# A third seven-product pair in each SwiGLU unit, eight in each half of the last product, and gate biases by DMA

## The chip, the cores and the metric

The kernel runs on one core of a Trainium2 chip. The metric is the device time of one execution in microseconds; of several runs the median is given.

## The reference

One decoder block on `x` of 256 rows (tokens) and 2048 columns in fp32. Its first part, a token mixer, isn't touched by the change except for one gate row. The second part is a SwiGLU feed-forward layer, with `D_FF` = 5632:

```
mod = silu(c) @ w_ada + b_ada
shift1, scale1, gate1, shift2, scale2, gate2 = split(mod, 6)
h = rms_norm(x, norm1_gain) * (1 + scale1) + shift1
x = x + gate1 * mixing_sublayer(h, ...)
h = rms_norm(x, norm2_gain) * (1 + scale2) + shift2
gate, up = split(h @ w_ffn_in, 2)
x = x + gate2 * ((silu(gate) * up) @ w_ffn_out)
```

`w_ffn_in` is 2048 x 11264, `w_ffn_out` 5632 x 2048, `w_ada` 2048 x 12288.

## The kernel before, in words

**Products in three matmuls.** Each fp32 operand is split into a high part (a cast) and a low part (what the cast left over). A product of a 128 x 128 block of activations with a 128 x 512 block of weights is three matmuls into one PSUM bank (`mm3`, L164 to L166): high by high, high by low, low by high. Weights stream from HBM by SP's DMA queue into `raw` (four buffers); ACT casts `whi`, DVE subtracts for `wlo` (four buffers each; L158 and L159 in `load_weights`, L1276 and L1277 in `load_pair`). A buffer of `whi` is free when PE's last matmul on it is done.

**SwiGLU units.** The columns of `w_ffn_in` are done in 11 units of 512 gate and 512 up columns each. The inner dimension has 16 blocks, or eight *pairs*; there are two token tiles. An ordinary pair is (2 blocks) x (gate, up) x (2 tiles) = 8 block products, 24 matmuls. Units 1 to 7 (`FAST`) go through `fast_products`, in the order of `PAIRS`, where a 1 marks a pair that is done with seven block products in the manner of Strassen and Winograd, 21 matmuls. Such a *fast* pair needs sums of weights (four subtractions on DVE, L1280, and split as well) and sums of activations (made once, by `sums_of_h2`). Four of its seven products go to shared banks `p1`, `p5`, `p7`, `p6`, which all fast pairs of a unit add into; behind the last fast pair `u`, `first` and `third` are formed from them (one copy on ACT, four operations on DVE), and `merge` adds them to the unit's four banks with four additions on DVE (L1311). `merge(0)` comes two pairs behind the last fast one and `merge(1)` three pairs behind; where no such pair is left, both come at the end. A unit has four banks of its own and four of the other kind; units alternate between `acc` and `misc`.

**Behind a unit** come its sigmoids on ACT (L1387), the gate products on DVE (L1388) and the products with the up half (L1399). The result is transposed on PE in the next unit behind its pair 0 (`turn`, L1115) and split (L191, L192 and their neighbours), so that it is a left operand of the last product.

**The last product** takes the 44 blocks of the result by `w_ffn_out`. Columns 0 to 1023 go by `OUT_A`, 22 pairs of which six are fast; columns 1024 to 2047 by `OUT_B`, 14 pairs of which six are fast, and then ordinary `block` calls for the rest. The left sums of the fast pairs come from three units (`OUT_UNITS`), by `sums_of_unit` (L1429 to L1439) at `hooks`, positions in `OUT_A`. `LOOK` is how many pairs ahead weights are loaded in `OUT_A`.

**Background work.** The gate rows `gate1` and `gate2` are made beside the products: `ada_segment_steps` loads pieces of `w_ada`, `mac` multiplies and adds them on DVE (L286 for the first, L288 for the others), and `rows_of` adds the bias, loaded by a DMA into a scratch row (L970), with four additions on DVE (L971), splits, sums over partitions by matmuls with ones (L985, L986) and copies. How many steps are taken for each pair or block is set by `RATE_MID` (gate1), `RATE_FFN` and, in the last product, `RATE_OUT` (gate2). `flush` takes all that is left.

**Order.** A scheduler sets the order on each engine from the program's order and priorities; `prio()` moves work ahead. Each engine then takes its instructions in that order.

Of the kernel before, what the change touches and what calls it, by code (L numbers as in the profile page):

```python
# [10 lines left out]
F32 = mybir.dt.float32  # L11
# [20 lines left out]
SEG_SHIFT1, SEG_SCALE1, SEG_GATE1, SEG_SHIFT2, SEG_SCALE2, SEG_GATE2 = range(6)  # L32
RATE_IN, RATE_MID, RATE_FFN = 0.8, 0.6, 0.65
RATE_OUT = 2.5
LOOK = 3
DEFER = 4
# [8 lines left out]
FAST = range(1, 8)  # L45
OUT_UNITS = (4, 5, 6)
OUT_A = tuple((p, 0) for p in range(7)) + tuple(x for i in range(6) for x in ((8 + i, 1), ((7, 14, 15, 16, 17, 18)[i], 0))) + (
    (19, 0), (20, 0), (21, 0))
OUT_B = ((0, 0), (1, 0)) + tuple(x for i in range(6) for x in ((8 + i, 1), (2 + i, 0)))
PAIRS = ((0, 0), (1, 0), (6, 1), (2, 0), (7, 1), (3, 0), (4, 0), (5, 0))  # L50
RANK = 16
# [25 lines left out]
def trunk(ctx: ExitStack, tc: tile.TileContext, I, out):  # L77
# [204 lines left out]

    def ada_mac(acc, raw, k):
        c = csil[:, k : k + 1]
        if k == 0:
            nc.vector.tensor_scalar(acc, raw, c, None, op0=ALU.mult)  # L286
        else:
            nc.vector.scalar_tensor_tensor(acc, raw, c, acc, op0=ALU.mult, op1=ALU.add)  # L288
# [69 lines left out]
    def mac():  # L358
        acc, j, k, raw, done = macs.pop(0)
        with tc.issue_after(state["split"].ins):  # L360
            ada_mac(acc[j], raw, k)
        if done is not None:
            after.append(done)

    def ada_segment_steps(acc, seg, done):


        for k in range(KC):
            for j in range(2):
                while len(macs) >= len(ring["tags"]):  # L370
                    mac()
                raw = araw([P, 2 * NB])
                c0 = seg * D + j * 2 * NB
                with prio():
                    nc.sync.dma_start(raw, w_ada[k * P : (k + 1) * P, c0 : c0 + 2 * NB])
                macs.append((acc, j, k, raw, done if (k, j) == (KC - 1, 1) else None))
                yield
# [587 lines left out]
    def rows_of(name, seg, acc):  # L965

        quarters = [a[:, c : c + NB] for a in acc for c in (0, NB)]
        for j, q in enumerate(quarters):
            br = scr([1, NB])
            nc.sync.dma_start(br, I["b_ada"][:, seg * D + j * NB : seg * D + (j + 1) * NB])  # L970
            nc.vector.tensor_add(q[0:1, :], q[0:1, :], br)  # L971
            yield
        for _ in range(4):
# [211 lines left out]
    def norm2_turn(t, xs):  # L1185
# [8 lines left out]
        for j, ps in enumerate(banks):  # L1194
            hf = S(f"T6", [P, 4, P]) if (j, t) == (3, 0) else scr([P, 4, P])
            h2_raw[j, t] = hf
# [171 lines left out]
    for i in range(NFF):  # L1368
# [54 lines left out]
    KF = 4 * NFF  # L1423
    CUT = KF - 14
    w_fo = I["w_ffn_out"]
    out_sums = {}

    def sums_of_unit(n):
# [5 lines left out]
        sums_of(sf, [full[:, :, t * P : (t + 1) * P] for t in range(NT)], slice(0, 4, 2), slice(1, 4, 2))  # L1434
        hi, lo = (S(f"H{2 + 2 * n + i}", [P, 4, 2, P], F32R) for i in range(2))
        nc.scalar.copy(hi, sf)
        nc.vector.tensor_tensor(lo, sf, hi.bitcast(F32), op=ALU.subtract)
        for m in range(2):
            out_sums[2 * e + m] = [(hi[:, j, m, :], lo[:, j, m, :]) for j in range(4)]  # L1439
# [62 lines left out]
```

## Time and profile before

| | |
|---|---|
| median of 3 runs | 1597.8 us (1597.12 to 1598.16) |
| profiled execution | 1597.22 us, of which the span is 1595.4 us |
| TensorE (PE) busy | 1582.0 us, 99% of the span |
| VectorE (DVE) busy | 1275.5 us, 80% |
| ScalarE (ACT) busy | 837.6 us, 53% |
| DMA | 395.97 MB, 248 GB/s in the mean |
| unit 1 begins, last product begins (from the trace) | at some 918 us and 1353 us of the span |

PE is TensorE's matmuls, PEld its weight loads; DVE is VectorE, ACT ScalarE, POOL GpSimd, SP SyncE, which issues the DMAs. L12 is line 12 of the kernel before. A row of a group reads: line, engine, operation, output and inputs with shape, count, busy time and mean ns of one, idle time ahead of it and who ended that. A row of a timeline gives start and duration in us. A row of stretches gives the busy time of each engine.

### The profile page before, as it was taken

What the parts mean: (1) busy time and instruction counts of PE and PEld (TensorE: products, weight loads), DVE (VectorE), ACT (ScalarE), POOL (GpSimd) and SP (SyncE); (2) the same over time, 40 slices, a digit from 0 to 9 for tenths busy, and PEclk for the clock granted to TensorE, in tenths of its full rate; (3) what the DMA queues carried; (4) which work ended last, traced back from release to release, by engine and by line L of the source; (5) the groups of instructions that cost most, each with busy time, mean ns of one, the idle gap of its engine ahead of it and who ended that gap; (6) DMA issues with size and microseconds to landing.
All of it is one profiled execution on the core that took longest, in us unless ns stands there. A gap on an engine that the chain in (4) does not pass through costs nothing.

```text
span 1595.4 us, 20167 instructions
## 1 busy us (share of the span) xinstructions
PE 1582.0 (99%) x7272; PEld 1308.2 (82%) x7272; DVE 1275.5 (80%) x1523; ACT 837.6 (53%) x1184; POOL 5.3 (0%) x14
## 2 busy tenths in 40 slices
PE   8999999999999999999999999999999999999998
PEld 7878888888888888888887888888888888778887
DVE  6889995888878787878756688888887677988884
ACT  5654449775754434444446655555454443554552
POOL 1000000000000000000000000000000000000000
PEclk9999999999999999999999999999999999999999
DMA  9999997667778889989766466556657889667664
GB/s 339 365 326 320 332 302 245 214 189 257 247 258 280 297 301 314 311 289 310 228 192 210 149 196 195 192 184 193 205 183 226 281 302 314 203 196 225 212 204 140
DMA packets 194596, 395.97 MB, mean 248 GB/s; under 512 B 12914, under 2 KB 27928, under 8 KB 194496
## 3 DMA queue, kind: packets, MB, share of 16 engines
q1 hardware_dynamic: 194096, 394.60, 75.0%
q8 instruction: 57, 0.93, 0.2%
q14 instruction: 43, 0.35, 0.1%
q10 hardware_dynamic: 176, 0.07, 0.0%
q0 software_dynamic: 224, 0.01, 0.0%
HBM read 392.53 MB, written 2.10 MB: 247 GB/s over the span
## 4 chain that ended last, share of the span: by engine, by line
PE 85%; DMA 5%; DVE 5%; ACT 3%; issue 2%; SPq 0%; ACTq 0%; DVEq 0%
PE acc L166 21%; PE acc L165 21%; PE acc L164 20%; PE misc L164 6%; PE misc L166 6%; PE misc L165 6%; DVE wlo L159 1%; ACT whi L158 1%; DMA AR<-w_ada 1%; DVE ada L288 1%; DMA raw<-w_br_gla 1%; DMA raw<-w_ffn_out 1%; PE acc L434 1%; DMA raw<-w_in 1%; PE misc L800 1%
## 5 line engine op out<-in xcount | busy, mean ns | idle before, releaser
L158 ACT CAST whi<-raw 128x1024 fp32r<-128x1024 f32 x362 | 368.6, 1022 | 412.2 <-PE acc L166 264.9
L159 DVE TENSOR_TENSOR wlo<-raw,whi 128x1024 fp32r<-128x1024 f32 x362 | 425.6, 1183 | 186.0 <-ACT whi L158 184.4
L164 PE MATMUL acc<-whi,H 128*128 128x512 f32 x1308 | 511.9, 392 | 1.2 <-ACT H L446 0.8
L165 PE MATMUL acc<-wlo,H 128*128 128x512 f32 x1308 | 510.9, 391 | 0.8 <-DVE wlo L159 0.7
L166 PE MATMUL acc<-whi,H 128*128 128x512 f32 x1308 | 509.8, 390 | 0.4 <-DVE H L453 0.4
L166 PEld LDWEIGHTS acc<-whi,H 128*128 128x128 f32 x1308 | 245.3, 188 | 52.9 <-DVE H L453 1.6
L164 PEld LDWEIGHTS acc<-whi,H 128*128 128x128 f32 x1308 | 245.5, 188 | 52.3 <-ACT H L446 1.3
L165 PEld LDWEIGHTS acc<-wlo,H 128*128 128x128 f32 x1308 | 245.7, 188 | 51.3 <-DVE wlo L159 1.7
L1276 ACT CAST whi<-raw 128x1024 fp32r<-128x1024 f32 (+1 forms) x184 | 179.2, 992 | 134.5 <-PE acc L166 68.0
L1277 DVE TENSOR_TENSOR wlo<-raw,whi 128x1024 fp32r<-128x1024 f32 (+1 forms) x184 | 205.2, 1145 | 19.8 <-ACT whi L1276 18.8
L164 PE MATMUL misc<-whi,H 128*128 128x512 f32 x246 | 96.1, 391 | 0.0
L165 PE MATMUL misc<-wlo,H 128*128 128x512 f32 x246 | 95.8, 389 | 0.0
L166 PE MATMUL misc<-whi,H 128*128 128x512 f32 x246 | 95.8, 389 | 0.0
L164 PE MATMUL acc<-whi,A 128*128 128x512 f32 x222 | 87.1, 394 | 0.5 <-ACT whi L1276 0.4
L165 PE MATMUL acc<-wlo,A 128*128 128x512 f32 x222 | 86.7, 390 | 0.8 <-DVE wlo L159 0.8
L166 PE MATMUL acc<-whi,A 128*128 128x512 f32 x216 | 84.3, 390 | 0.0
L288 DVE SCALAR_TENSOR_TENSOR ada<-AR,csil,ada 128x1024 f32<-128x1024 f32 x59 | 74.8, 1278 | 3.6 <-DMA AR<-w_ada 3.6
L165 PEld LDWEIGHTS misc<-wlo,H 128*128 128x128 f32 x246 | 46.2, 188 | 9.7 <-DVE wlo L1277 0.2
L166 PEld LDWEIGHTS misc<-whi,H 128*128 128x128 f32 x246 | 46.2, 188 | 9.5
L164 PEld LDWEIGHTS misc<-whi,H 128*128 128x128 f32 x246 | 46.2, 188 | 9.5
L164 PEld LDWEIGHTS acc<-whi,A 128*128 128x128 f32 x222 | 41.7, 188 | 9.6 <-ACT whi L1276 1.1
L165 PEld LDWEIGHTS acc<-wlo,A 128*128 128x128 f32 x222 | 41.7, 188 | 9.6 <-DVE wlo L159 1.1
(428 smaller groups left out, 1927.6 us busy)
## 6 DMA issues: line engine op xcount, KB each, us to landing
raw<-w_in SPq DMA_DIRECT2D x205, 512.0 KB, 4.8
raw<-w_ffn_in SPq DMA_DIRECT2D x176, 512.0 KB, 4.2
raw<-w_ffn_out SPq DMA_DIRECT2D x88, 512.0 KB, 4.8
AR<-w_ada SPq DMA_DIRECT2D x79, 512.0 KB, 5.1
raw<-w_out SPq DMA_DIRECT2D x32, 512.0 KB, 4.8
KC<-w_ada SPq DMA_DIRECT2D x30, 512.0 KB, 6.2
OS<-w_ada SPq DMA_DIRECT2D x16, 512.0 KB, 6.9
KD<-w_ada SPq DMA_DIRECT2D x16, 512.0 KB, 5.8
```

Source lines behind the costliest of these rows:

```text
L158: state["cast"] = nc.scalar.copy(hi[:, :n, :], raw[:, :n, :])
L159: state["split"] = nc.vector.tensor_tensor(lo[:, :n, :], raw[:, :n, :], hi[:, :n, :].bitcast(F32), op=ALU.subtract)
L164: nc.tensor.matmul(ps, lh, rh, start=start, stop=False, skip_group_check=seeded)
L165: nc.tensor.matmul(ps, lh, rl, start=False, stop=False, skip_group_check=seeded)
L166: state["mm"] = nc.tensor.matmul(ps, ll, rh, start=False, stop=stop, skip_group_check=seeded)
L288: nc.vector.scalar_tensor_tensor(acc, raw, c, acc, op0=ALU.mult, op1=ALU.add)
L434: state["warm"] = nc.tensor.matmul(ps, ones_r, wide, start=True, stop=True)
L800: nc.tensor.matmul(ps[:n, t * N_GLA + h, :].rearrange("p (s l) -> p s l", l=L), at(f, h, t)[:, :n], odd(at(f, h, t)), start=True, stop=True,)
L1276: nc.scalar.copy(hi[:, :n, :], src)
L1277: state["split"] = nc.vector.tensor_tensor(lo[:, :n, :], src, hi[:, :n, :].bitcast(F32), op=ALU.subtract)
```

## The change

Each fast unit gets a third fast pair (pair 5), and the fast pairs stand at positions 2, 4 and 6 of 0 to 7 instead of 2 and 4. `OUT_UNITS` gets a fourth unit; `OUT_A` and `OUT_B` have eight fast pairs each, `OUT_B` now covers 32 of the 44 blocks, and the rest of the third and fourth column blocks goes by ordinary blocks as before. The left sums are put into other tiles, some of them in pieces, and are made at positions 0, 2, 6 and 9 of `OUT_A` instead of 1, 2 and 4; `flush` moves from position 7 to 4. The sums of h2 get those of pair 5 and stand ahead of unit 0's gate products. For both gates the accumulators are set to zero by GpSimd and their row 0 is filled with the bias by DMA; the first multiply then also adds, and the four bias additions go. `RATE_FFN` goes from 0.65 to 0.75, `LOOK` from 3 to 2. PE's matmuls go from 7106 to 7073, DVE's instructions from 1525 to 1600 in the program.

```diff
-RATE_IN, RATE_MID, RATE_FFN = 0.8, 0.6, 0.65
+RATE_IN, RATE_MID, RATE_FFN = 0.8, 0.6, 0.75
-LOOK = 3
+LOOK = 2
...
-OUT_UNITS = (4, 5, 6)
-OUT_A = tuple((p, 0) for p in range(7)) + tuple(x for i in range(6) for x in ((8 + i, 1), ((7, 14, 15, 16, 17, 18)[i], 0))) + (
-    (19, 0), (20, 0), (21, 0))
-OUT_B = ((0, 0), (1, 0)) + tuple(x for i in range(6) for x in ((8 + i, 1), (2 + i, 0)))
-PAIRS = ((0, 0), (1, 0), (6, 1), (2, 0), (7, 1), (3, 0), (4, 0), (5, 0))
+OUT_UNITS = (3, 4, 5, 6)
+OUT_A = tuple((p, 0) for p in range(5)) + tuple(x for i in range(8) for x in ((6 + i, 1), ((5, *range(14, 21))[i], 0))) + ((21, 0),)
+OUT_B = tuple((p, int(6 <= p < 14)) for p in (0, 1, 6, 2, 7, 8, 3, 9, 4, 10, 11, 5, 12, 14, 13, 15))
+PAIRS = ((0, 0), (1, 0), (5, 1), (2, 0), (6, 1), (3, 0), (7, 1), (4, 0))
...
-    def ada_mac(acc, raw, k):
+    def ada_mac(acc, raw, k, zero=True):
         c = csil[:, k : k + 1]
-        if k == 0:
+        if k == 0 and zero:
...
+    def biased(acc, seg):
+        for j, a in enumerate(acc):
+            nc.gpsimd.memset(a, 0.0)
+            with prio():
+                nc.sync.dma_start(a[0:1, :], I["b_ada"][:, seg * D + j * 2 * NB : seg * D + (j + 1) * 2 * NB])
+        return acc
...
-        for j, q in enumerate(quarters):
-            br = scr([1, NB])
-            nc.sync.dma_start(br, I["b_ada"][:, seg * D + j * NB : seg * D + (j + 1) * NB])
-            nc.vector.tensor_add(q[0:1, :], q[0:1, :], br)
-            yield
...
-                acc = [S(f"T{4 + j}", [P, 2 * NB]) for j in range(2)]
-                yield from ada_segment_steps(acc, seg, rows_of("gate1", seg, acc))
+                acc = biased([S(f"T{4 + j}", [P, 2 * NB]) for j in range(2)], seg)
+                yield from ada_segment_steps(acc, seg, rows_of("gate1", seg, acc), False)
...
-        acc = halves(S("ada", [P, D]))
-        yield from ada_segment_steps(acc, SEG_GATE2, rows_of("gate2", SEG_GATE2, acc))
+        acc = biased(halves(S("ada", [P, D])), SEG_GATE2)
+        yield from ada_segment_steps(acc, SEG_GATE2, rows_of("gate2", SEG_GATE2, acc), False)
...
     def sums_of_h2():
         out = {}
-        sf = S("KC", [P, 4, 2, P])
+        sf = S("AR1", [P, 4, P])
+        sums_of(sf.rearrange("p s (n d) -> p s n d", n=1), [h2_raw[2, t] for t in range(NT)], slice(2, 3), slice(3, 4))
+        hl = S("AR0", [P, 2, 4, P], F32R)
+        nc.scalar.copy(hl[:, 0], sf)
+        nc.vector.tensor_tensor(hl[:, 1], sf, hl[:, 0].bitcast(F32), op=ALU.subtract)
+        out[5] = [(hl[:, 0, j, :], hl[:, 1, j, :]) for j in range(4)]
+        sf = S("AR1", [P, 4, 2, P])
...
+        if i == 0:
+            h2s = sums_of_h2()
         sgs = []
...
-        if i == 0:
-            h2s = sums_of_h2()
...
-    CUT = KF - 14
+    CUT = 2 * len(OUT_B)
...
+    rooms = [S(f"H{2 + j}", [P, 4, 2, P], F32R) for j in range(6)]
...
-        hi, lo = (S(f"H{2 + 2 * n + i}", [P, 4, 2, P], F32R) for i in range(2))
-        nc.scalar.copy(hi, sf)
-        nc.vector.tensor_tensor(lo, sf, hi.bitcast(F32), op=ALU.subtract)
+        homes = []
+        for part in range(2):
+            own = act[e][part][:, 0:4:2, P:T]
+            if n < 3:
+                rest = [(rooms[2 * n + part][:, 0:3], slice(1, 4))]
+            else:
+                rest = [(rooms[2 * j + part][:, 3:4], slice(1 + j, 2 + j)) for j in range(3)]
+            homes.append([(own, 0)] + rest)
+        for part in range(2):
+            for (dst, c), (hi, _) in zip(homes[part], homes[0]):
+                if part == 0:
+                    nc.scalar.copy(dst, sf[:, c])
+                else:
+                    nc.vector.tensor_tensor(dst, sf[:, c], hi.bitcast(F32), op=ALU.subtract)
...
-    hooks = {at: (lambda n=n: sums_of_unit(n)) for n, at in enumerate((1, 2, 4))}
-    hooks[7] = flush
+    hooks = {at: (lambda n=n: sums_of_unit(n)) for n, at in enumerate((0, 2, 6, 9))}
+    hooks[4] = flush
...
-    REST = 2 * len(OUT_B)
-    block(o[0], act_at, w_fo, REST, KF, 2 * NB, go_on=True, seeded=True)
+    block(o[0], act_at, w_fo, CUT, KF, 2 * NB, go_on=True, seeded=True)
...
-    block(pss, act_at, w_fo, REST, CUT, n * NB, go_on=True, more=True, seeded=True)
```

More of the change, by code (lines that the diff above doesn't have):

```diff
@@ L358, in mac, with ada_segment_steps @@
     def mac():
-        acc, j, k, raw, done = macs.pop(0)
+        acc, j, k, raw, done, zero = macs.pop(0)
         with tc.issue_after(state["split"].ins):
-            ada_mac(acc[j], raw, k)
+            ada_mac(acc[j], raw, k, zero)
         if done is not None:
             after.append(done)
-    def ada_segment_steps(acc, seg, done):
+    def biased(acc, seg):
[4 more added lines that the diff above has]
+        return acc
+    def ada_segment_steps(acc, seg, done, zero=True):
         for k in range(KC):
@@ L375, in ada_segment_steps @@
                     nc.sync.dma_start(raw, w_ada[k * P : (k + 1) * P, c0 : c0 + 2 * NB])
-                macs.append((acc, j, k, raw, done if (k, j) == (KC - 1, 1) else None))
+                macs.append((acc, j, k, raw, done if (k, j) == (KC - 1, 1) else None, zero))
                 yield
@@ L1194, in norm2_turn @@
         for j, ps in enumerate(banks):
-            hf = S(f"T6", [P, 4, P]) if (j, t) == (3, 0) else scr([P, 4, P])
+            hf = S(("KC", "T6")[j - 2], [P, 4, P]) if t == 0 and j >= 2 else scr([P, 4, P])
             h2_raw[j, t] = hf
@@ L1434, in sums_of_unit @@
         sums_of(sf, [full[:, :, t * P : (t + 1) * P] for t in range(NT)], slice(0, 4, 2), slice(1, 4, 2))
-        hi, lo = (S(f"H{2 + 2 * n + i}", [P, 4, 2, P], F32R) for i in range(2))
-        nc.scalar.copy(hi, sf)
-        nc.vector.tensor_tensor(lo, sf, hi.bitcast(F32), op=ALU.subtract)
-        for m in range(2):
-            out_sums[2 * e + m] = [(hi[:, j, m, :], lo[:, j, m, :]) for j in range(4)]
+        homes = []
[12 more added lines that the diff above has]
+                    nc.vector.tensor_tensor(dst, sf[:, c], hi.bitcast(F32), op=ALU.subtract)
+        for m in range(2):
+            views = []
+            for part in range(2):
+                v = [homes[part][0][0][:, m, :]]
+                for dst, _ in homes[part][1:]:
+                    v += [dst[:, j, m, :] for j in range(dst.shape[1])]
+                views.append(v)
+            out_sums[2 * e + m] = list(zip(*views))
     state["rate"] = RATE_OUT
-    hooks = {at: (lambda n=n: sums_of_unit(n)) for n, at in enumerate((1, 2, 4))}
-    hooks[7] = flush
+    hooks = {at: (lambda n=n: sums_of_unit(n)) for n, at in enumerate((0, 2, 6, 9))}
+    hooks[4] = flush
     o = fast_products(w_fo, 0, NB, OUT_A, act_at, out_sums, acc_bank, misc_bank, ("AR0", "AR1"), hooks)
```

## The prediction

> **What bounds the kernel now.** I read the page of the profile first, from its head to the chain that ended last.
>
> ```profile
> span 1595.4 us, 20167 instructions
> PE 1582.0 (99%) x7272; PEld 1308.2 (82%) x7272; DVE 1275.5 (80%) x1523; ACT 837.6 (53%) x1184; POOL 5.3 (0%) x14
> PEclk9999999999999999999999999999999999999999
> PE 85%; DMA 5%; DVE 5%; ACT 3%; issue 2%; SPq 0%; ACTq 0%; DVEq 0%
> ```
>
> PE is busy in 99% of the span at an unthrottled clock, and the chain is PE's in 85%. A matmul taken out is therefore worth its full issue time, as long as PE is fed; a stall put in costs its full length. Next I read PE itself: the chain of waits through the SwiGLU units, where each unit transposes its predecessor's result right behind its own pair 0, then PE's timeline at such a place, and PE's waits from 1200 us on.
>
> ```profile
> 1052.95 0.87 PE misc L1115 x8
> 1096.02 0.88 PE acc L1115 x8
> ...
> 1269.65 0.87 PE misc L1115 x8
> 1314.07 0.87 PE misc L1115 x8
> ...
> 1052.79 1.03 PE L1115 MATMUL misc<-ident,scr 128*128 128x128 f32 x8
> ...
> PE misc L985 <- ACT T L980: 0.8, 1, 0.8
> PE acc L164 <- ACT whi L1276: 0.4, 1, 0.4
> ```
>
> A fast unit takes 1096.02 - 1052.95 = 43.07 us and an ordinary one 1314.07 - 1269.65 = 44.42. Fast units have two pairs of 21 matmuls and six of 24, 186 in all; ordinary ones have 192. Less the 0.87 of transposes, that is 42.20/186 = 43.55/192 = 0.227 us a matmul. Two sorts of unit with the same quotient means that neither stalls. The two waits are all that PE shows in the last 395 us, both in the last product.
>
> What the change leans on is DVE, so I asked for the busy time in unit 3 and in two stretches at the start of the last product, and for the groups by form.
>
> ```profile
> 1004.40:1047.45 43.05, 43.05 (x196) 35.73 (x195) 36.16 (x43) 22.36 (x25) 0.00 (x0) 1.00 0.61 197
> 1350.00:1400.00 50.00, 48.92 (x221) 38.95 (x219) 46.12 (x60) 24.42 (x32) 0.00 (x0) 1.00 0.64 208
> 1400.00:1450.00 50.00, 49.45 (x216) 40.29 (x216) 44.40 (x50) 28.89 (x32) 0.00 (x0) 1.00 0.68 212
> ...
> L1277 DVE TENSOR_TENSOR wlo<-raw,whi 128x1024 fp32r<-128x1024 f32 x129 | 153.3, 1220 | 12.0 <-ACT whi L1276 11.1
> L1280 DVE TENSOR_TENSOR AR<-raw,AR 128x512 f32<-128x512 f32 x24 | 16.5, 687 | 0.3
> L971 DVE TENSOR_TENSOR ada<-ada,scr 1x512 f32<-1x512 f32 x4 | 2.6, 673 | 0.0
> L1251 DVE TENSOR_TENSOR AR<-AR,AR 128x256 f32<-128x256 f32 x6 | 2.5, 416 | 0.0
> L1432 DVE TENSOR_TENSOR AR<-T,T 128x1024 f32<-128x1024 f32 x2 | 2.4, 1216 | 0.0
> ```
>
> After the engine sums the columns are PE, PEld, DVE, ACT. DVE is busy 36.2 of 43.05 us in a unit; in the last product 46.1 and 44.4 of 50, and there PE loses 1.1 and 0.55 us.
>
> **Matmuls removed.** Each further fast pair takes three matmuls away. Seven units gain one each: 7 x 3 x 0.227 = -4.8 us. The last product goes from 6 + 6 to 8 + 8: 4 x 3 x 0.227 = -2.7 us. [...]
>
> **DVE inside a unit.** Here are DVE's and ACT's own rows around the end of unit 3.
>
> ```profile
> 1046.18 0.69 DVE L1399 TENSOR_TENSOR scr<-scr,misc 128x512 f32<-128x512 f32 x1
> 1046.79 1.22 DVE L1277 TENSOR_TENSOR wlo<-raw,whi 128x1024 fp32r<-128x1024 f32 x1
> 1047.92 0.68 DVE L1399 TENSOR_TENSOR scr<-scr,misc 128x512 f32<-128x512 f32 x1
> 1048.63 1.23 DVE L1277 TENSOR_TENSOR wlo<-raw,whi 128x1024 fp32r<-128x1024 f32 x1
> 1049.77 0.69 DVE L1280 TENSOR_TENSOR OD<-raw,raw 128x512 f32<-128x512 f32 x1
> 1050.37 0.69 DVE L1280 TENSOR_TENSOR OD<-raw 128x512 f32<-128x512 f32 x1
> ...
> 1044.82 0.60 ACT L1387 ACTIVATE scr<-misc 128x512 f32<-128x512 f32 x1 [0.76 <-PE misc L166]
> 1045.32 1.04 ACT L1276 CAST whi<-raw 128x1024 fp32r<-128x1024 f32 x1
> 1047.54 1.05 ACT L1276 CAST whi<-raw 128x1024 fp32r<-128x1024 f32 x1 [1.18 <-PE misc L166]
> ```
>
> From start to start a split of 1024 takes DVE 1.13 us (1046.79 to 1047.92) and an operation on 512 0.60 (1049.77 to 1050.37). An ordinary pair needs two splits, 2.3 us; a fast one three splits of 1024, one of 512 and four subtractions, 3.4 + 5 x 0.60 = 6.4. So a fast and an ordinary pair together need 8.7 us of DVE in (21 + 24) x 0.227 = 10.2 us of PE. The third fast pair lifts DVE from 36.2 to about 40.3 of 42.4 us a unit. Followed operation by operation through the alternation, the splits land 0.5 to 1.2 us ahead of their matmul: it fits, at no cost, and it would cost at once if an operation of DVE took 10% longer.
>
> **The unit's end: the main term.** The last fast pair moves from position 4 to position 6 of 0 to 7. The four additions that merge the shared banks then no longer fit between pairs; they come behind the unit's last matmul, and the gate's two and the product's two multiplications behind them. In DVE's order of the changed program the split of the *second half* of the next unit's pair 0 stands behind all of these; before, both halves' splits stood ahead of the last gate product, as the rows show (1046.79). DVE takes its rows in that order, so the split waits for what waits for PE's last matmul.
>
> Set the unit's end at 0. Before, it was 24 x 0.227 = 5.45 us ahead of the transposes at 1052.79, at 1047.34; ACT's cast released by that matmul starts at 1047.54, so a result is seen 0.2 us later. Then: last merge 0.2 to 0.8; first gate product to 1.4. The second waits for its sigmoid. On ACT that sigmoid stands behind a cast whose buffer PE's last matmul frees: cast 0.2 to 1.25 (1.05), sigmoid to 1.85 (0.60). Second gate product 1.9, the two others 2.5 and 3.1, the split 3.7 to 4.93 (1.23). PE meanwhile has the 12 matmuls of the first half and four high-part ones which the program's order puts ahead: 16 x 0.227 = 3.63. It stalls 4.93 - 3.63 = 1.3 us. The trace of before holds no such stall, so the bounds are these: if the sigmoid isn't held by the cast, products follow each other at 0.60 and the stall is 0.9; with 0.69 for each instead of 0.60 it is 1.6. I take 1.3. The same order stands at the six ends of units 1 to 6: 7.8 us. At the end of unit 7 only two matmuls are put ahead, so 1.3 + 2 x 0.227 = 1.75. Together +9.55 us (6.75 to 11.7).
>
> [...]
>
> **The last product.** Gate2's row: four bias additions of 0.67 go (2.7 us of DVE), and the higher rate moves some of its multiply-adds into the units. Of the 1.6 us that PE lost in the two stretches, I give back 0.8 (0 to 1.6). Left sums: now four, at hooks 0, 2, 6, 9. One costs DVE 1.2 + 4 x 0.42 + 1.2 = 4.1 us, and the pieces in which it is now written make it 4.2 to 4.5. The first two fall among ordinary pairs, which leave DVE 3.2 us each. The last two fall among alternating pairs, where 1.5 us is spare and splits lead by up to 1.2 to 1.9 us: 4.3 - 1.5 - 1.9 = 0.9, and 1.0 for the one in four pieces. In the second half two fast pairs stand twice without an ordinary one between; two need 12.8 us of DVE in 9.5 of PE, of which leads and the pair before cover most; I put 0.45 on each (0 to 1.5). Sum: -2.7 - 0.8 + 1.9 + 0.9 = -0.7 us (-3 to +2).
>
> **Biases and the rest.** The first multiply-add of each half becomes one that also adds:
>
> ```profile
> L288 DVE SCALAR_TENSOR_TENSOR ada<-AR,csil,ada 128x1024 f32<-128x1024 f32 x59 | 74.8, 1278 | 3.6 <-DMA AR<-w_ada 3.6
> 462.24 0.75 DVE L286 TENSOR_SCALAR T<-AR,csil 128x1024 f32<-128x1024 f32 x1
> 245.92 1.04 POOL L605 CAST KC<-T 128x1024 uint8<-128x1024 f32 x1 [240.92 <-DMA T<-k_lvl]
> 455.47 0.29 SPq L970 DMA_DIRECT2D scr<-b_ada  x1
> ...
> 905.83 1.23 DVE L159 TENSOR_TENSOR wlo<-raw,whi 128x1024 fp32r<-128x1024 f32 x1 [1.50 <-ACT whi L158]
> ```
>
> That is +0.53 us twice for each gate, against -2.7. No memset by POOL of that size is in the trace; its nearest row is a cast of 1.04 us, and POOL is idle 99.7% of the span, so four cost nothing unless SP waits for one. The new bias DMA waits for the memset, and behind it on SP stand weight loads; the tiles are free long before, so I take no wait there, and the waiting DMAs of L970 go away. For gate1 in the middle of the kernel, where PE is fed, I put -0.3 (-1 to +0.5). The sums of pair 5 (four operations on 128 and a split of 512, some 1.8 us) fall in unit 0, whose up half leaves DVE idle for 1.50 us ahead of a split (the row at 905.83); nothing.
>
> **Sum**, against the profiled execution (1597.22 us: the span and 1.8 around it; 0.6 under the median, within the three runs' spread of 1.04): -4.8 + 9.55 - 0.7 - 0.3 = +3.75, so **1601.0 us**. About 0.2%, 3.2 us, is what a measurement of this kernel can tell from no change: faster is under 1594.6, slower over 1601.0. My forecast lies on the upper bound.
>
> **Rivals.** *The unit's end doesn't stall*, the side opposite to the forecast: the sigmoid and the products keep to DVE's gaps, or PE's queue holds more work than the 16 matmuls I count. Then -4.8 - 0.7 - 0.3 = -5.8, 1591.4 us. For it: in before no unit's end stalls though products stand there too. Against it: there, the splits are ahead. It decides at 5.8/7 = 0.8 us an end, where the change is worth nothing. Chance 0.22.
>
> *A small stall and a better last product*: 0.9 at six ends and 1.35 at the seventh (6.75), the last product at -1.5: -4.8 + 6.75 - 1.5 - 0.3 = +0.15, 1597.4. For it: in unit 3 both sigmoids found ACT free (1044.82). Against it: a cast starts with PE's last matmul (1047.54), and in the changed order the second sigmoid stands behind that cast. Chance 0.14.
>
> *DVE becomes the bound in the alternation too*: its spare 0.5 us before an ordinary pair is eaten by 10% longer operations, 0.9 us per fast and ordinary pair, twice in each unit behind the first: if a quarter of these 14 places loses 0.9 us and the back-to-back pairs lose 1.5, that is +3.2 + 2.1 = +5.3, 1606.3. For it: DVE at 95% of the unit. Against it: the same fast and ordinary pair alternate in unit 3 already, and its quotient of 0.227 leaves no room for a loss. Chance 0.19.
>
> **Numbers.** The forecast's own case has 0.45. The last product can go wrong further up than down (-3 to +2 about -0.7) and the stall about as far both ways, so I spread it evenly from 1598.2 to 1605.2; 0.6 of that lies over 1601.0. Slower: 0.6 x 0.45 + 0.19 of the third rival = 0.46. Within 0.2%: the other 0.18, and 0.12 of the second rival = 0.30. Faster: the first rival's 0.22 and 0.02 of the second = 0.24. The range runs from 1591.5 to 1606.0: about half of the first rival, whose last product has the same bounds, and about half of the third lie outside, 2 in 10.
>
> **What would show it.** Right: the fast units' transposes 43.7 us apart instead of 43.07; at each end of a unit a wait of PE for DVE's wlo of L1286, 1.3 us each and some 9 in all; in DVE's timeline, four multiplications after the merge and the split behind them. Wrong: units of 42.4 us without such a wait (first rival); waits inside the units instead (third); a wait for w_ada's DMA or SP behind a memset. In the last product I expect some 3 us of PE's waits for wlo, at the hooks 6 and 9 and at the pairs back to back.

## The result, and the profile after

The changed kernel takes 1619.73 us (median of 4 runs, 1615.37 to 1621.1) against 1597.98 us before (4 runs, 1597.12 to 1598.81): 1.0128 times the time, 95% interval 1.0112 to 1.0144. It is slower, as forecast, but by 21.8 us and not by the 3.75 of the forecast's sum, and lies far outside the range of 1591.5 to 1606.0. The profiled execution took 1620.12 us with a span of 1618.3, so 22.9 us of span are to be explained. The page of the changed kernel, the same lines as were shown of before:

```profile
span 1618.3 us, 20207 instructions
PE 1585.0 (98%) x7239; PEld 1300.8 (80%) x7239; DVE 1320.6 (82%) x1598; ACT 855.3 (53%) x1214; POOL 9.1 (1%) x18
PEclk9999999999999999999999999999999999999999
PE 72%; DVE 12%; DMA 9%; ACT 4%; issue 3%; SPq 0%; DVEq 0%; ACTq 0%
```

PE has 33 matmuls fewer and is still the busiest engine, but its share of the chain that ended last fell from 85 to 72%, and DVE's rose from 5 to 12%. PE now waits. The waits of PE from 900 us to the end (before, the two rows that the prediction shows from 1200 us on are all there was from 900 us on):

```profile
PE misc L164 <- DVE wlo L1286: 8.0, 8, 1.5
PE acc L164 <- DVE wlo L1286: 4.6, 6, 1.1
PE misc L988 <- ACT T L983: 4.6, 1, 4.6
PE acc L164 <- DVE wlo L158: 1.9, 2, 1.6
PE misc L163 <- ACT whi L1285: 1.3, 4, 0.6
PE acc L163 <- ACT whi L1285: 1.0, 4, 0.3
```

I placed the 22.9 us by PE's transposes (L1118 here, L1115 before), as in the prediction:

| stretch | before | after | difference | forecast |
|---|---|---|---|---|
| start to unit 1's transposes | 923.59 | 925.01 | +1.4 | -0.3 |
| seven fast units | 301.46 | 314.59 | +13.1 | +4.8 |
| from there to the end of the span | 370.35 | 378.70 | +8.35 | -0.7 |

**The units.** A unit took 44.94 us in the mean (44.30 to 45.59) where I had forecast 43.7. Each has two stalls, not one. The first is the one of the prediction. PE, ACT and DVE around the end of unit 2, timelines (start, duration, and in brackets the idle time ahead and who ended it):

```profile
1009.87 1.07 PE L163 MATMUL misc<-whi,H 128*128 128x512 f32 x4
1012.04 0.50 PE L164 MATMUL misc<-wlo,H 128*128 128x512 f32 x1 [1.10 <-DVE wlo L1286]
...
1007.39 1.05 ACT L1285 CAST whi<-raw 128x1024 fp32r<-128x1024 f32 x1 [1.15 <-PE acc L165]
1008.35 0.59 ACT L1398 ACTIVATE scr<-acc 128x512 f32<-128x512 f32 x1
...
1007.35 0.70 DVE L1320 TENSOR_TENSOR acc<-acc,KC 128x512 f32<-128x512 f32 x1
1007.96 0.68 DVE L1399 TENSOR_TENSOR scr<-scr,acc 128x512 f32<-128x512 f32 x1
1008.97 0.69 DVE L1399 TENSOR_TENSOR scr<-scr,acc 128x512 f32<-128x512 f32 x1 [0.34 <-ACT scr L1398]
1009.58 1.28 DVE L1408 TENSOR_TENSOR scr<-scr,acc 128x512 f32<-128x512 f32 x2
1010.77 4.63 DVE L1286 TENSOR_TENSOR wlo<-raw,whi 128x1024 fp32r<-128x1024 f32 x4
```

The unit's last matmul ends 16 matmuls ahead of 1009.87 + 4 x 0.227 = 1010.78, at 1007.15. The last merge, the four products (the second held by its sigmoid, the sigmoid by a cast that PE's last matmul released) and the split follow in the order of the prediction. PE issues the four high-part matmuls at 1009.87 and then stands until the split's first piece is done. It loses 1.26 us there and 0.11 in the matmul behind: 1.37 at each of the six ends between fast units, 1.83 at the end of unit 7, 10.05 together; the forecast was 9.55.

The second stall wasn't forecast. It comes once in each unit, where the ordinary pair behind the first fast pair begins. DVE, SP and PE in unit 3, which begins there:

```profile
1019.51 0.68 DVE L1289 TENSOR_TENSOR KD<-raw,KD 128x512 f32<-128x512 f32 x1
1020.11 1.22 DVE L1286 TENSOR_TENSOR wlo<-OD,whi 128x1024 fp32r<-128x1024 f32 x1
...
1024.88 0.69 DVE L1289 TENSOR_TENSOR OD<-raw,raw 128x512 f32<-128x512 f32 x1 [1.81 <-DMA raw<-w_ffn_in]
1025.49 3.49 DVE L1286 TENSOR_TENSOR wlo<-raw,whi 128x1024 fp32r<-128x1024 f32 x3
...
1020.23 0.37 SPq L1278 DMA_DIRECT2D raw<-w_ffn_in  x1
...
1026.76 0.50 PE L164 MATMUL misc<-wlo,H 128*128 128x512 f32 x1 [1.28 <-DVE wlo L1286]
```

The first fast pair's last subtraction on its weights ends at 1020.2; that frees the buffer of `raw`, and SP issues the transfer for the second fast pair at 1020.23. It is there 4.65 us later. DVE has the second fast pair's first subtraction at the head of its queue and stands 1.81 us until those weights are there. Behind it stands the split of the ordinary pair that comes *sooner* on PE, whose own weights are ready. PE waits 1.28 us for that split, and starts when its first piece is done. DVE's waits of this kind from 926 to 1225 us, first the changed kernel, then the kernel before (two in each of six units of the changed kernel; the other of the two is at the first fast pair's own first subtraction, 1.10 us in this unit):

```profile
DVE OD L1289 <- DMA raw<-w_ffn_in: 13.6, 12, 1.8
...
DVE OD L1280 <- DMA raw<-w_ffn_in: 0.2, 1, 0.2
```

The order was the same before, but there the weights had landed when DVE came to the subtraction. Before, at the start of unit 4, whose transposes are at 1052.79:

```profile
1052.71 0.68 DVE L1280 TENSOR_TENSOR KD<-raw,KD 128x512 f32<-128x512 f32 x1
1053.46 0.37 SPq L1269 DMA_DIRECT2D raw<-w_ffn_in  x1
...
1059.00 0.69 DVE L1280 TENSOR_TENSOR OD<-raw,raw 128x512 f32<-128x512 f32 x1
```

There the first fast pair's last subtraction ended 0.6 us behind the start of the transposes, and DVE came to the next pair's first one 5.5 us after the transfer's issue. In the changed kernel it ended 5.7 us behind them (1020.19, transposes at 1014.45), since DVE had come to this pair late from the unit's end, and DVE came to the next one after 2.8 us.

PE's loss at that place was 0.66, 0.62, 1.54, 0.46, 1.80, 1.01 and 1.20 us in units 1 to 7: 7.3 us. It hangs on when a transfer lands, and so differs between executions: with the units written the same, the seven took 315.0 us in `units_only`'s profiled execution and 320.0 in `rate65`'s (both below). So the units give -4.8 + 10.05 + 7.3 = +12.55 of the measured 13.1.

**The last product's start.** PE's single longest wait stands here: gate2's first row matmul (L988), which the scheduler put ahead of the last product's first matmul. PE, DVE, ACT and SP, and then the stretches around it (columns after the engine sums: PE, PEld, DVE, ACT, POOL, granted clock, DMA share, GB/s):

```profile
1373.13 0.58 PE L988 MATMUL misc<-T,ones_r 128*128 128x256 f32 x1 [4.58 <-ACT T L983]
1373.51 0.63 PE L163 MATMUL acc<-whi,A 128*128 128x512 f32 x1
1373.94 0.63 PE L164 MATMUL acc<-wlo,A 128*128 128x512 f32 x1
...
1359.00 2.54 DVE L158 TENSOR_TENSOR wlo<-raw,whi 128x1024 fp32r<-128x1024 f32 x2 [2.20 <-ACT whi L157]
1363.16 1.23 DVE L158 TENSOR_TENSOR wlo<-raw,whi 128x1024 fp32r<-128x1024 f32 x1 [1.62 <-ACT whi L157]
1364.31 1.28 DVE L288 SCALAR_TENSOR_TENSOR ada<-AR,csil,ada 128x1024 f32<-128x1024 f32 x1
...
1371.35 1.29 DVE L288 SCALAR_TENSOR_TENSOR ada<-AR,csil,ada 128x1024 f32<-128x1024 f32 x1 [1.10 <-DMA AR<-w_ada]
...
1362.08 1.05 ACT L157 CAST whi<-raw 128x1024 fp32r<-128x1024 f32 x1 [1.80 <-DMA raw<-w_ffn_in]
...
1349.84 0.33 SPq L383 DMA_DIRECT2D AR<-w_ada  x1
...
1365.61 0.34 SPq L383 DMA_DIRECT2D AR<-w_ada  x1
...
1365.00:1368.00 3.00, 3.00 (x15) 2.49 (x14) 3.00 (x4) 2.11 (x2) 0.00 (x0) 1.00 0.90 238
1373.00:1376.00 3.00, 2.87 (x7) 2.37 (x8) 3.00 (x4) 1.02 (x2) 0.00 (x0) 0.50 0.63 226
```

The row matmul needs the sum over all of gate2's pieces of `w_ada`. Three buffers serve these pieces, and SP issues the last piece that the row needs at 1365.61, when the multiply-add of 1364.31 has freed its buffer. That multiply-add's own piece had been issued at 1349.84; it stood in DVE's queue behind splits of weights, for whose casts DVE had waited 2.20 and 1.62 us, and the cast ahead of the latter had waited 1.80 us for its weights. The last piece is there 5.7 us after its issue, and the multiply-add, the cast and the matmul follow. Behind the wait PE runs at half its clock: 0.43 us from matmul to matmul (1373.51 to 1373.94) for seven matmuls, 1.4 us lost. With 0.8 us of waits for weights at the end of unit 10 the start of the last product loses 7.0 us. Further on it loses 3.5 us at the sums of positions 6 and 9 (1419 and 1440 us) and 2.2 us at the two places where fast pairs stand back to back (1526 and 1552 us). Before, this stretch lost some 3.4 us, all in gate2's row. So -2.7 + 7.0 + 3.5 + 2.2 - 3.4 = +6.6 of the measured 8.35; the rest is spread over gaps too small to place.

### The profile page after: what moved, and what is told of

It reads as the page before. It is cut to its first block, busy times and chain, and to the rows that moved or that the text cites. A ratio compares the mean times of both kernels' runs of the same rounds, so it can differ in the third digit from the quotient of the medians.

```text
span 1618.3 us, 20207 instructions
## 1 busy us (share of the span) xinstructions
PE 1585.0 (98%) x7239; PEld 1300.8 (80%) x7239; DVE 1320.6 (82%) x1598; ACT 855.3 (53%) x1214; POOL 9.1 (1%) x18
## 4 chain that ended last, share of the span: by engine, by line
PE 72%; DVE 12%; DMA 9%; ACT 4%; issue 3%; SPq 0%; DVEq 0%; ACTq 0%
PE acc L164 18%; PE acc L165 18%; PE acc L163 18%; DMA raw<-w_ffn_in 5%; DVE wlo L1286 4%; PE misc L164 4%; PE misc L165 4%; PE misc L163 4%; DMA AR<-w_ada 2%; DVE wlo L158 1%; DVE AR L1289 1%; DVE ada L288 1%; DMA raw<-w_ffn_out 1%; ACT whi L157 1%; DMA raw<-w_br_gla 1%
## 5 line engine op out<-in xcount | busy, mean ns | idle before, releaser
L157 ACT CAST whi<-raw 128x1024 fp32r<-128x1024 f32 x358 | 364.3, 1021 | 404.3 <-PE acc L165 233.5
L158 DVE TENSOR_TENSOR wlo<-raw,whi 128x1024 fp32r<-128x1024 f32 x358 | 421.2, 1184 | 172.7 <-ACT whi L157 170.6
L163 PE MATMUL acc<-whi,H 128*128 128x512 f32 x1294 | 505.3, 392 | 1.7 <-ACT H L454 0.8
L165 PE MATMUL acc<-whi,H 128*128 128x512 f32 x1294 | 504.4, 390 | 0.4 <-DVE H L461 0.4
L163 PEld LDWEIGHTS acc<-whi,H 128*128 128x128 f32 x1294 | 242.9, 188 | 53.8 <-ACT whi L1285 1.4
L165 PEld LDWEIGHTS acc<-whi,H 128*128 128x128 f32 x1294 | 242.7, 188 | 52.0 <-DVE H L461 1.6
L1285 ACT CAST whi<-raw 128x1024 fp32r<-128x1024 f32 (+1 forms) x188 | 176.7, 967 | 82.1 <-PE acc L165 32.1
L164 PE MATMUL misc<-wlo,H 128*128 128x512 f32 x225 | 89.0, 395 | 7.5 <-DVE wlo L1286 7.5
L165 PE MATMUL misc<-whi,H 128*128 128x512 f32 x225 | 87.7, 390 | 0.0
L163 PE MATMUL misc<-whi,H 128*128 128x512 f32 x225 | 86.4, 391 | 0.9 <-ACT whi L1285 0.9
L163 PE MATMUL acc<-whi,A 128*128 128x512 f32 x216 | 85.3, 395 | 0.2 <-ACT whi L157 0.2
L165 PE MATMUL acc<-whi,A 128*128 128x512 f32 x208 | 81.5, 392 | 0.0
L1285 ACT CAST whi<-AR 128x1024 fp32r<-128x1024 f32 x32 | 33.7, 1053 | 52.7 <-DVE AR L1289 47.4
L1286 DVE TENSOR_TENSOR wlo<-AR,whi 128x1024 fp32r<-128x1024 f32 x32 | 39.2, 1225 | 17.5 <-ACT whi L1285 17.4
L163 PEld LDWEIGHTS misc<-whi,H 128*128 128x128 f32 x225 | 42.2, 188 | 10.5 <-ACT whi L1285 1.8
L165 PEld LDWEIGHTS misc<-whi,H 128*128 128x128 f32 x225 | 42.3, 188 | 8.3
```

The source lines that it names most:

```text
L157: state["cast"] = nc.scalar.copy(hi[:, :n, :], raw[:, :n, :])
L158: state["split"] = nc.vector.tensor_tensor(lo[:, :n, :], raw[:, :n, :], hi[:, :n, :].bitcast(F32), op=ALU.subtract)
L163: nc.tensor.matmul(ps, lh, rh, start=start, stop=False, skip_group_check=seeded)
L164: nc.tensor.matmul(ps, lh, rl, start=False, stop=False, skip_group_check=seeded)
L165: state["mm"] = nc.tensor.matmul(ps, ll, rh, start=False, stop=stop, skip_group_check=seeded)
L1285: nc.scalar.copy(hi[:, :n, :], src)
```

## The experiments

The medians of each comparison are from the same chip; that of before lay between 1597.7 and 1599.2 us. Intervals are 95%.

**Which part costs what.** Four kernels with one part of the change undone, or that part alone.

`units_only`: the third fast pair alone, on the kernel before.

```diff
-PAIRS = ((0, 0), (1, 0), (6, 1), (2, 0), (7, 1), (3, 0), (4, 0), (5, 0))
+PAIRS = ((0, 0), (1, 0), (5, 1), (2, 0), (6, 1), (3, 0), (7, 1), (4, 0))
...  (and the sums for pair 5)
```

> The kernel before with only the third fast pair of units 1 to 7 (its order of pairs, the sums for pair 5). Theory A (two stalls in each unit: 1.4 us at its end, where the next split stands behind the gate products, and about 1.0 us in its first fast pair, where DVE waits for a late weight transfer): -4.8 + 10.0 + 7.3 = +12.5, about 1610 us, units 44.9 us apart. Rival B (only the stall at the unit's end belongs to the third pair, the other comes from elsewhere in the change): -4.8 + 10.0 = +5, about 1603 us, units 43.8 us apart.

Measured: 1613.61 against 1599.23 us, ratio 1.0094 (1.0072 to 1.0117). The units of the profiled execution (1611.38 us) are 44.46 to 45.85 us apart, 45.00 in the mean. Theory A holds: both stalls belong to the third pair.

`two_fast`: the change without it.

```diff
-PAIRS = ((0, 0), (1, 0), (5, 1), (2, 0), (6, 1), (3, 0), (7, 1), (4, 0))
+PAIRS = ((0, 0), (1, 0), (6, 1), (2, 0), (7, 1), (3, 0), (4, 0), (5, 0))
```

> The changed kernel with the units' order of pairs as before (two fast pairs, at positions 2 and 4); all else changed. Theory A: the units are back at 43.07 us and what is left is the last product's start and its fast pairs, about 1620 - 13 = 1607 us. Rival B (the late transfer in the first fast pair isn't due to the third pair): units of about 44.1, 1614 us.

Measured: 1607.0 us, ratio 1.0053 (1.0038 to 1.0068). All seven units are 43.05 to 43.08 us apart, as before the change. Theory A again; 8 us are left, most of it in the last product.

`bias_only`: the biases by DMA alone, on the kernel before.

> The kernel before with only the gate biases by DMA into accumulators that GpSimd sets to zero. Theory A: within 1 us of before, 1597 to 1599 us. Rival B (the 1.4 us by which the changed kernel is late already where unit 1 begins come from SP waiting behind the memsets): 1599 to 1600 us, unit 1 begins 1.4 us later.

Measured: 1598.87 against 1599.23 us, ratio 1.0002 (0.9992 to 1.0011). No difference: theory A. Unit 1's transposes come at 925.01 in its profile, 1.4 us late as in the changed kernel. That isn't shown to come from the biases. SP does wait behind memsets, 4.0 us in two, but at 886 us of the span (gate2's accumulators), and PE is as late already at 872 us. And kernels that are written as the changed one is up to there have the transposes from 922.54 (`split_ahead`) to 925.31 us (`gate2_no_loads`), which is more than 1.4 us of difference between one execution and another.

`rate65`: gate2's rate and flush as before.

```diff
-RATE_IN, RATE_MID, RATE_FFN = 0.8, 0.6, 0.75
+RATE_IN, RATE_MID, RATE_FFN = 0.8, 0.6, 0.65
...
-    hooks[4] = flush
+    hooks[7] = flush
```

> The changed kernel with gate2's work at its rate of before (0.65 instead of 0.75) and flushed at position 7 instead of 4. Theory A (the first matmul of gate2's row stands in PE's queue ahead of the last product and waits there 4.6 us for a late transfer of w_ada, and the matmuls behind run at half pace for a while): this goes, some 6 us faster than the changed kernel, about 1614 us. Rival B (the wait comes from the two pairs of look-ahead instead of three, or from the sums at position 0, which stay): no faster than 1618 us.

Measured: 1619.99 us, ratio 1.0126 (1.0109 to 1.0142): nothing gained that can be measured. In its profile the wait at L988 is down from 4.6 to 1.6 us, but PE waits 1.1 us at the next row matmul and 1.6 us for weights behind it. Theory A had the wait's place right; of the gain of 6 us, the profile has 3.6 from unit 8's transposes on (375.1 us instead of 378.7). But it is of a run of 1625.68 us, the longest of four, which against the changed kernel's lost 5.4 us in the units and 3.7 ahead of them, and a gain of that size can't be told from runs that spread over 8.0 us here and 5.7 in the changed kernel.

**The two stalls in a unit: order or work?**

`subs_behind`: a fast pair's first two subtractions are queued behind the last split of the pair ahead.

```diff
+            prev = state["split"].ins
             r0, r1 = raw_at(c0), raw_at(c1)
...
-            sub(ta[:, 0], r1[:, 0], r0[:, 0])
-            sub(ta[:, 1], r1[:, 1], r1[:, 0])
+            with tc.issue_after(prev):
+                sub(ta[:, 0], r1[:, 0], r0[:, 0])
+                sub(ta[:, 1], r1[:, 1], r1[:, 0])
```

> The changed kernel, but the first two subtractions of every fast pair are queued on DVE behind the last split of the pair ahead of it, so that a late transfer of their weights holds up nobody else's split. Theory A (DVE stands at a subtraction whose weights are late while PE waits for a split queued behind it): the 7.3 us of stalls in the units' first fast pairs go, the 1.4 us at the ends stay, units of 43.8 us, about 1612 us. Rival B (the splits are late since DVE is short of time, not since it waits): units stay at 44.9 us, 1619 us.

`split_ahead`: the next fast unit's pair 0 is loaded and split ahead of the merge.

```diff
             load(n + LOOK)
+            if n == end - 1 and pre:
+                pre()
...
+        def pre():
+            state["next"] = [load_pair(w_ff, PAIRS[0][0], (i + 1) * NB, DFF + (i + 1) * NB, 0, None)]
```

> The changed kernel, but the next fast unit's pair 0 is loaded and split ahead of the merge and the gate products of the unit before. In its order on DVE the subtractions of the second fast pair also come behind the splits of the ordinary pair ahead of it. Theory A (both stalls in a unit are matters of order on DVE, not of too much work): both go at the six ends between fast units, units of 42.4 to 42.8 us, about -14 us against the changed kernel, 1605 us. Rival B (DVE has no room for a third fast pair, and the delay only moves to a later split): units of 43.6 us or more, 1613 us or more.

PE's waits from 926 to 1225 us, first in `subs_behind`, then in `split_ahead`; and two successive transposes of each:

```profile
PE acc L164 <- DVE wlo L1286: 3.3, 3, 1.1
PE misc L164 <- DVE wlo L1286: 3.3, 3, 1.1
...
1013.04 1.03 PE L1118 MATMUL acc<-ident,scr 128*128 128x128 f32 x8
1056.83 1.03 PE L1118 MATMUL misc<-ident,scr 128*128 128x128 f32 x8
```

```profile
PE acc L164 <- DVE wlo L158: 1.6, 1, 1.6
...
964.94 1.03 PE L1118 MATMUL misc<-ident,scr 128*128 128x128 f32 x8
1007.33 1.04 PE L1118 MATMUL acc<-ident,scr 128*128 128x128 f32 x8
```

`subs_behind`: 1615.67 against 1598.28 us, ratio 1.0115 (1.009 to 1.0141). The six waits that are left are those of the ends, 1.1 us each, and units are 43.79 us apart: the 43.7 of the prediction. The whole kernel gains less than the units do: its interval overlaps the changed kernel's. In its profile the seven units are 7.5 us shorter, but the time from there to the end is 3.8 us longer (382.5 instead of 378.7). The edit acts on the last product's fast pairs too: PE loses some 4.2 us at those that stand back to back, where it lost 2.2. `split_ahead`: 1604.47 us, ratio 1.0042 (1.0027 to 1.0057). Units are 42.39 us apart, which is 183 x 0.227 and the 0.87 of transposes: not a stall is left but the one at the end of unit 7, which this kernel doesn't touch. DVE does the same work in both, 1319 us, and 1320.6 in the changed kernel; so both stalls are matters of the order on DVE. That `split_ahead` also ends the second one is due to its order, in which the subtractions stand behind the ordinary pair's splits.

**The last product's start: transfers or DVE?**

`split_rate100`: `split_ahead` with `RATE_FFN` at 1.0.

> The kernel split_ahead with gate2's work at rate 1.0 instead of 0.75, so that its loads of w_ada end well ahead of the last product. Theory A (PE stands at gate2's first row matmul until a late transfer of w_ada has been added, and then runs at half pace for seven matmuls): both go, 5 to 6 us faster than split_ahead, about 1599 us. Rival B (the transfers compete with the weights and the wait only moves, to weights in units 8 to 10): no gain, units 8 to 10 longer than 44.43 us.

Measured: 1603.39 us, ratio 1.0034 (1.002 to 1.0048), within `split_ahead`'s interval. The 4.7 us at L988 are gone (1.1 and 0.3 us at L989 are left), but PE stands for 1.73 us and shorter times for weights in unit 9, which takes 50.52 us to its transposes instead of 44.43. Rival B: the loss moved.

`ahead_rate65`: both repairs of the units, unit 8's first weights as well, and the rate and flush of `rate65`.

> The changed kernel with both repairs of the units (unit 8 too), and gate2's work at rate 0.65 with its flush at position 7, as before. Theory A (the rate makes the wait at the last product's start): against the kernel split_ahead 1.8 us at unit 8 and some 3 to 5 us at the last product's start go, about 1598 us. Rival B (the wait only moves into the last product, where flush now meets fast pairs): 1602 us.

Measured: 1603.8 against 1598.87 us, ratio 1.0035 (1.0021 to 1.0048). Rival B: PE waits 1.9 us at L988, with slow matmuls behind, and 1.0 us at the last product's first matmul some 8 us ahead of it, and more for weights among the fast pairs; some 4.2 us at those back to back, as in `subs_behind`, whose edit it has.

`out_only`: the units' order, the rate, the flush and `LOOK = 3` as before, so that of the change the last product and the biases are left.

> The changed kernel with the units' order of pairs, gate2's rate, its flush and the look-ahead as before: what is left of the change is the last product with eight and eight fast pairs, its sums, and the biases by DMA. Theory A (twelve matmuls fewer, -2.7 us, against 3.3 us of stalls at the sums of positions 6 and 9 and 2.1 us at the fast pairs back to back): 1 to 4 us slower than before, about 1600.5 us. Rival B (those stalls come from gate2's work or the shorter look-ahead): -2.7 us, about 1595.5 us.

Measured: 1605.98 us, ratio 1.005 (1.0036 to 1.0064): 7.1 us, more than theory A allowed. In the last product PE waits 3.0 us at L988 in two parts, with slow matmuls behind the first, and loses 4.8 us at the sums and 2.1 at the back-to-back pairs, where 3.3 and 2.1 were expected. Theory A's places are right; L988's wait stays at the old rate too. Two kernels tried to shift these, with one edit each on `out_only`: `enumerate((0, 1, 3, 4))` for the sums' positions, and `range(8)` for the four empty steps in `rows_of`.

> The kernel out_only with the left sums made at positions 0, 1, 3 and 4 of the last product instead of 0, 2, 6 and 9, so that none falls between fast pairs. Theory A (a set of sums between fast pairs delays their splits): the 4.1 us of waits at the two places go, about 1602.5 us. Rival B (DVE has no room for them at the start either, beside gate2's row): the waits come back ahead of the first fast pair, no gain, 1606 us.

> The kernel out_only with four more steps of waiting ahead of gate2's row, in place of the four steps that the bias additions took. Theory A (without those steps the row's first matmul is queued too soon, ahead of the transfers that it waits for): its wait of 2.0 us, the seven slow matmuls behind it and the second wait of 1.0 us go, about 1602 us. Rival B (the transfers of w_ada are late, whatever the steps): the wait stays, 1606 us.

Measured: 1607.47 against 1597.73 us, ratio 1.006 (1.0037 to 1.0084), and 1610.42 us, ratio 1.007 (1.0052 to 1.0087). Rival B in both: with early sums the waits of the sums shrink, but gate2's row waits four times at L988, 4.1 us; with late steps the row's waits add up to 3.5 us in five parts. By then it was open what is short there, DVE or the transfers. Two kernels on `split_ahead` take one away and leave the other. The row's first matmul (L988, L991 in these two) stands directly ahead of the last product's first one in both, as in `split_ahead`.

`gate2_no_loads`:

```diff
-                raw = araw([P, 2 * NB])
...
+                if seg == SEG_GATE2 and k:
+                    raw = state["raw", j]
+                else:
+                    raw = state["raw", j] = araw([P, 2 * NB])
...
```

> The kernel split_ahead without 30 of the 32 transfers of w_ada for gate2 (its multiply-adds all run, on the two pieces that are loaded); the row's first matmul stands at the same place in PE's order. Theory A (the row's matmul waits for late transfers): the wait of 4.7 us, the slow matmuls behind it and the waits for weights at the end of unit 10 go, about 8 us less, 1597 us. Rival B (DVE is short of time at the last product's start): the wait stays, 1604 us.

`gate2_short_macs`:

```diff
-            ada_mac(acc[j], raw, k, zero)
+            if "rows2" in state and k:
+                ada_mac(acc[j][:, :16], raw[:, :16], k, zero)
+            else:
+                ada_mac(acc[j], raw, k, zero)
...
+        state["rows2"] = True
```

> The kernel split_ahead with all of gate2's transfers, but 30 of its 32 multiply-adds cut to 16 columns, so that they cost DVE almost nothing. Theory A (late transfers): the wait at the row's first matmul stays, since the transfers are as late, 1603 us or more. Rival B (DVE is short of time): it goes, about 1597 us.

PE's waits from 1310 us on, first without the loads, then with the short multiply-adds; and of the latter DVE's time with SP's issue for it:

```profile
PE misc L163 <- ACT whi L1288: 1.3, 4, 0.5
PE acc L163 <- ACT whi L1288: 1.0, 4, 0.3
PE misc L164 <- DVE wlo L1289: 0.6, 1, 0.6
PE acc L163 <- DVE acc L1323: 0.2, 1, 0.2
```

```profile
PE misc L992 <- DVE T L987: 4.0, 3, 1.7
...
PE misc L991 <- ACT T L986: 0.6, 1, 0.6
...
1342.31 5.15 DVE L158 TENSOR_TENSOR wlo<-raw,whi 128x1024 fp32r<-128x1024 f32 x4 [6.42 <-ACT whi L157]
1347.38 0.23 DVE L288 SCALAR_TENSOR_TENSOR ada<-AR,csil,ada 128x16 f32<-128x16 f32 x1
1347.63 0.34 SPq L386 DMA_DIRECT2D AR<-w_ada  x1
1354.45 0.23 DVE L288 SCALAR_TENSOR_TENSOR ada<-AR,csil,ada 128x16 f32<-128x16 f32 x1 [4.15 <-DMA AR<-w_ada]
```

Without the loads: 1597.68 against 1598.9 us, ratio 0.9996 (0.9987 to 1.0006), where `split_ahead` has 1.0042, some 7 us less; no wait of gate2's row is left, and none for weights at the end of unit 10, where `split_ahead` loses 1.8 us. With the short multiply-adds: 1605.92 us, ratio 1.0045 (1.0028 to 1.0061), no gain: DVE stands idle for 4.15 us until the piece of `w_ada` is there, 6.8 us after its issue. The issue waited for the multiply-add of 1347.38, which costs next to nothing now and still stood behind splits for whose casts DVE had waited 6.42 us. The first row matmul waits only 0.6 us, where theory A had its wait stay; the next ones wait 4.0 us in its place. So it is the transfers and not the work of the multiply-adds: both theories had a time for each kernel, and theory A's fit. Whether the weights come late by their place in SP's queue or by the share that `w_ada` takes of the DMA engines, these two don't separate.

**A version that beats both.** `units_ahead` is the kernel before with the third fast pair, both repairs, and unit 8's first weights (four blocks) split ahead as well; the last product, the biases and gate2 are those of before.

> The kernel before with the third fast pair in units 1 to 7, the first weights of the next unit (unit 8 too) split ahead of the merge and the gate products, and the first two subtractions of a fast pair queued behind the split ahead of them; last product, biases and gate2's rate as before. Theory A (the third pair is worth its 21 matmuls once both stalls are gone): units of 42.39 us, -4.8 us in all, about 1593 us where before has 1597.5 to 1598.5. Rival B (work that was put ahead is late elsewhere: at unit 8 or in the last product): less than 2 us gained.

```profile
PE 1577.6 (99%) x7251; PEld 1304.8 (82%) x7251; DVE 1301.1 (82%) x1570; ACT 848.5 (53%) x1199; POOL 5.3 (0%) x14
```

Measured: 1595.01 us (11 runs, 1592.11 to 1595.62) against 1598.87 (15 runs, 1597.56 to 1600.36), ratio 0.9976 (0.9967 to 0.9985). PE has no wait in the seven units, which are 42.37 to 42.40 us apart. Theory A gave 1593; it is 3.9 us faster than before. The row shown is of the run of 1592.11 us.

## Why the prediction was wrong

The sign was right, the size was not, and the time lies 13.7 us above the range. Of the 19.1 us by which the profiled span grew more than forecast, 9.05 lie from unit 8's transposes on, 8.4 in the seven units and 1.7 ahead of them.

*Matmuls removed*: right. Where nothing stalls, a fast unit is 42.39 us (`split_ahead`), 0.68 less than before, three matmuls of 0.227.

*The unit's end*: right in mechanism, order and size: 1.37 us measured for 1.3, 1.83 for 1.75. The first rival (no stall) and the second (0.9) are out. The stall hangs on DVE's order: with the same split put ahead in the queue (`split_ahead`), units are 42.39 us and the stall is gone. Nor did a ready split pass a waiting row in the changed kernel: DVE stood 1.81 us at the subtraction of 1024.88, and the split behind it started at 1025.49.

*DVE inside a unit*: this step failed. "The splits land 0.5 to 1.2 us ahead of their matmul: it fits, at no cost" counted DVE's operations and took the weights as present. The same order that made the main term was not applied to the row of DVE in which a subtraction for a later pair stands ahead of a split for a sooner one. The subtraction's weights can't be there in time: their buffer is freed by the previous fast pair's last subtraction, a transfer takes 4.6 us, and DVE, late from the unit's end, comes to them 2.8 us after its issue. That is 7.3 us; `subs_behind` shows the cause in the units, which are 43.79 us apart without it. The third rival had waits at the right place with the wrong reason: operations longer by 10%. They aren't (a split takes 1.13 us from start to start, as before); `split_ahead` has the same operations and no wait.

*The last product*: this step failed too, with -0.7 forecast and +8.35 measured. I gave gate2's row a gain of 0.8 us since DVE would have less to do. But less work on DVE didn't help the row (`gate2_short_macs` took 1605.92 us, `split_ahead` 1604.47): what costs is the transfers of `w_ada`, which share SP's queue and the DMA engines with the weights (`gate2_no_loads` against `gate2_short_macs`; from 1310 to 1355 us the engines were busy 0.87 of the time in `split_ahead` and 0.60 without the loads). The prediction looked at DVE's busy share there and never at the landing times, though it had named a wait for `w_ada`'s DMA as a sign of being wrong. The row's first matmul also comes sooner in PE's order, and the transfers don't: before, it stood 87 instructions of PE behind the last product's first, without the bias additions 58 (`bias_only`, `out_only`), and with the higher rate and the earlier `flush` as well it stands ahead of it. That term is 7.0 us where the row lost 3.4 before. The sums at positions 6 and 9 cost 3.5 us for 1.9, the back-to-back pairs 2.2 for 0.9: terms with the right place and half the size or less. Most of PE's waits there are for ACT's casts (L1285) and not for `wlo` as forecast.

*Biases*: nothing that can be measured by themselves (`bias_only`), where -0.3 was forecast; SP did wait behind a memset, 4.0 us in two for gate2's accumulators at 886 us, where I took no wait; PE lost nothing by it.

## What to carry to other kernels

When a change makes an engine's queue tighter, write down the queue's order and, for each operation at its head, when *all* its operands can be there, the transfer's landing counted from the moment that its buffer is freed; busy shares don't show a ready operation that stands behind a waiting one. A stall of that kind is cured by moving a few instructions in the queue, which is why the same third fast pair cost 14 us in one order and won 3.9 in another. Background work that is paid by transfers had a latest and an earliest rate here: in `split_rate100`, sooner, PE waited for weights instead, up to 1.73 us, and in the changed kernel, later, gate2's row stood in PE's queue for 4.58 us.

## What the runs showed of the hardware

After PE had stood for 4.6 us its clock was granted at 0.50 for some 3 us (the stretch from 1373 to 1376 us), and seven 512-wide matmuls came 0.43 us apart; from 1376 to 1380 us it was granted at 0.98, and they came 0.23 us apart again. Slow matmuls also followed waits of 4.7 us (`split_ahead`, eleven matmuls), 3.8 (`two_fast`, seven), 2.0 us (`out_only`, seven, beginning 1.2 us after the wait), 1.9 us (`ahead_rate65`) and 1.73 us (`split_rate100`); in `rate65` they followed waits of 2.04 and 1.79 us inside two units, and in `out_sums_early` four waits of 1.09, 0.49, 0.28 and 1.15 us, which ended from 1387.43 to 1390.96 us. None of the stalls of 1.1 to 1.6 us at the units' ends was followed by slow matmuls, and neither were those of 1.75 us (`units_only`) and 1.70 (`gate2_short_macs`), so the length of one wait alone doesn't decide it.
